# Even layer of a residual trunk: rounded products for the input projection, conditioning columns on TensorE's column groups, and a shared convolution

## The chip, the cores and the metric

The kernel runs on one core of a Trainium2 chip. The core has TensorE (matrix products into PSUM; PE in the profile, with its weight loads apart as PEld), VectorE (DVE), ScalarE (ACT), GpSimd (POOL) and SyncE (SP), whose queue issues the weight transfers. The metric is the device time of one execution in microseconds (us), the median of several runs; less is better.

## The reference

Two residual layers over 256 tokens of 2048 features, all in float32. Each layer is conditioned by a vector c:

```python
c_act = jax.nn.silu(c)
for l in range(2):
    mod = c_act @ ada_w[l] + ada_b[l]          # ada_w[l]: 2048 x 12288
    shift1, scale1, gate1, shift2, scale2, gate2 = jnp.split(mod, 6, axis=-1)
    h = rms(x, norm1_g[l]) * (1 + scale1) + shift1
    mix = even_mixer(h, ...) if l % 2 == 0 else mla_mixer(h, ...)
    x = x + gate1 * mix
    h = rms(x, norm2_g[l]) * (1 + scale2) + shift2
    x = x + gate2 * (square(relu(h @ mlp_w1[l])) @ mlp_w2[l])
```

The even mixer (layer 0) projects h by a matrix of 2048 x 4096 and splits the result into u, v, a, g of 1024 columns. Mixer A gates u by a 128 x 128 causal product over v. Mixer B takes a * sigmoid(g), a causal depthwise convolution of 31 taps over 1024 channels, a LayerNorm and a swish. Both results go through one output projection of 2048 x 2048. The odd mixer (layer 1) is attention with low-rank queries and keys. The change is in the even layer and the conditioning that it needs.

## The kernel before

The weights stream from memory as tiles of 1 MiB (128 partitions x 2048 floats) through four buffers named `raw`, in the order in which the program asks for them. For almost all products a tile is split: ScalarE casts it to a rounded value `wh` (line 94), VectorE forms the rest `wl` (line 95), and TensorE adds up three rounded products, high by high, low by high and high by low (lines 183 to 185, and 210 to 212 at the start of an MLP). The activations are kept as such pairs too.

The input projection of the even layer is the exception. `gemm32` (line 153) takes the raw tile and the activations `x` as whole float32, one product for each block of 128 features, 128 tokens and 512 columns. Its tiles go through the `wh` buffers, so that seven 1 MiB buffers are open to transfers there. The program first brings the columns of shift1 and scale1, four quarters of 512 features each; as soon as a quarter is known, `norm_quarter` normalizes and transposes 512 features of x, and three of the eight column chunks (`pa`, `pg`, `pa1`) take them. The other five chunks follow, four tiles each.

The conditioning is work "beside the weight tiles": each weight tile calls `side_work`, which pops steps of one 1 MiB piece of `ada_w` from a queue at a given rate, and taps of the convolution.

- shift1 and scale1, and later shift2 and scale2, are column sums on VectorE (`ada_quarters`, line 269: four multiply-adds of 512 for each piece, into `accq`), then four transposes and a reduction.
- gate1 is a row (`ada_row` with `side`): ScalarE multiplies (line 302), GpSimd adds (line 303). The first quarter of shift2 and scale2 goes the same way (lines 263 and 265). The rest of shift2 and scale2 reaches into the start of the MLP, which waits for it quarter by quarter.
- The convolution is 248 multiply-adds of 256 tokens on VectorE (lines 540 and 542), read from a copy in PSUM, ten to a weight tile.

The order of the instructions on each engine is set by a scheduler that takes the program's steps as they become ready; the queues `ada_queue` and `conv_queue` set where the steps stand in the program. PSUM has eight banks: four for products (`mm`), two for transposes (`tr`), two others (`ms`).

Of the kernel before, what the change touches and what calls it, by code (L numbers as in the profile page):

```python
# [36 lines left out]
R0, R1, R2, R4 = 1.2, 0.8, 0.75, 0.4  # L37
RA, NA = 2.5, 4
# [4 lines left out]
class Trunk:  # L43
    def __init__(self, ctx, tc, t):
# [12 lines left out]
        self.ms = pool("ms", 2, space=bass.MemoryType.PSUM)  # L57
# [4 lines left out]
        self.first = 0  # tiles still to be split by GpSimd  # L62
        self.conv_rate = 10
        self.conv_y = {}
        self.quarters = {}

# [1 line left out]
    def rsqrt(self, out, v):  # L68
        """out = v ** -0.5 for v > 0: a first guess from the bits, a third-order step, a Newton step."""
# [14 lines left out]
        # out <- 8/3 of its third-order step, then Newton with the 8/3 taken out again  # L84
# [7 lines left out]
    def split(self, src, hi, lo, engine=None):  # L92
        """src = hi + lo, both with the 12 significant bits that one pass of the array takes."""
        self.nc.scalar.copy(hi, src)  # L94
        (engine or self.nc.vector).tensor_tensor(lo, src, hi.bitcast(F32), op=ALU.subtract)  # L95
# [6 lines left out]
    def transpose4(self, srcs):  # L102
        """Up to four [128, n] blocks -> one PSUM bank, transposed side by side."""
# [20 lines left out]
    def wtile(self, w, k0, nk, n0, nw):  # L124
# [3 lines left out]
        # VectorE is busy with the norm when a phase's first tiles come: GpSimd splits those  # L128
# [6 lines left out]
    def side_work(self, size=1.0):  # L135
        """Work that is spread beside the weight tiles: conditioning and the convolution."""
# [7 lines left out]
        for _ in range(min(self.conv_rate, len(self.conv_queue))):  # L144
            self.conv_queue.pop(0)()

    def gemm32(self, ps, x, w, g, n0):
        """ps += x[:, 512 features of group g] @ w[those, n0:n0+512], whole float32 passes."""
        raw = self.wraw(w, 4 * g, 4, n0, 512, whole=True)
        self.side_work()  # L150
        for h in range(NH):
            for k in range(4):
                self.nc.tensor.matmul(  # L153
                    ps[h], x[:, 4 * g + k, h * P : (h + 1) * P], raw[:, k, :],
                    start=g + k == 0, stop=4 * g + k == KB - 1,
                )
# [68 lines left out]
    def ada_col(self, layer, j):  # L225
        """self.mod[layer, j] = [128, 16], feature-major."""
# [19 lines left out]
    def ada_quarters(self, layer, j0, side=None, aided=0):  # L246
        """Columns j0 and j0 + 1 side by side, complete for 512 features after every eight steps.
        The first aided quarters go by ScalarE and GpSimd, with room for products in side."""
# [3 lines left out]
        def step(q, g, i):  # L252
            if (q, g, i) == (0, 0, 0):
                box["acc"] = self.tmp.tile([P, 2, 2, 512], F32, tag="acc", name="accq", bufs=1)
                for j in (j0, j0 + 1):
                    self.mod[layer, j] = self.const.tile([P, KB], F32, tag=f"mod{layer}{j}", name=f"mod{layer}{j}")
            acc = box["acc"][:, q % 2, i, :]
            raw = self.wraw(self.t["ada_w"][layer], 4 * g, 4, (j0 + i) * D + q * 512, 512)
            for k in range(4):
                c = self.cT[:, 4 * g + k : 4 * g + k + 1]  # L260
                if q < aided:
                    prod = acc if g + k == 0 else side[:, D + k * 512 : D + (k + 1) * 512]
                    nc.scalar.activation(prod, raw[:, k, :], AF.Copy, scale=c)
                    if g + k:
                        nc.gpsimd.tensor_tensor(acc, acc, prod, op=ALU.add)
                elif g + k == 0:
                    nc.vector.tensor_scalar(acc, raw[:, k, :], c, None, op0=ALU.mult)
                else:
                    self.last = nc.vector.scalar_tensor_tensor(acc, raw[:, k, :], c, acc, op0=ALU.mult, op1=ALU.add).ins  # L269
            if g == 3:  # L270
                self.ada_finish_col(self.mod[layer, j0 + i], layer, j0 + i, q, acc)
                if i == 1:
                    self.quarters[layer, j0] = q + 1
# [4 lines left out]
    def ada_row(self, layer, j, side=None):  # L278
        """self.mod[layer, j] = [128, 2048], the same in every partition. With side = [128, 4096],
# [744 lines left out]
```

## Time and profile before

| what | us |
|---|---|
| median of 3 runs (2189.74 to 2189.92) | 2189.75 |
| span of the profiled execution, first to last instruction | 2185.9 |
| what lies around the span, against the median | 3.85 |
| conditioning and three chunks, up to the last quarter of features | 0 to 132.45 |
| the rest of the input projection | 132.45 to 297.80 |
| mixers and output projection | 297.80 to 411.20 |
| start of the MLP of layer 0, up to its second matrix | 411.20 to 523.70 |
| the rest: MLP of layer 0, layer 1 | 523.70 to 2185.9 |

The mean granted TensorE clock is 0.987 of full speed. In the profile's rows the first number is a start or a busy time, as the sentence ahead says; "x4" counts instructions; an arrow in brackets names what the engine waited for. A float32 product is shown as two records of TensorE and two of its weight load, a rounded product as one of each. Where a row says "idle before", an engine that doesn't set the end may idle at no cost.

### The profile page before, as it was taken

The numbers are of one execution on the slowest core, as the hardware profiler recorded it, in microseconds if no ns is written. First come the engines' busy times: TensorE is split into PE (matmuls) and PEld (weight loads), VectorE is DVE, ScalarE is ACT, GpSimd is POOL, SyncE is SP. The second block draws the span as 40 slices with busy tenths as digits, with TensorE's granted clock in tenths as the row PEclk, the third lists the DMA queues.
The fourth block names the chain that finished last, engine by engine and source line by source line (L and its number), as shares of the span: only waits on it lengthen the run. The fifth ranks groups of instructions, "written<-read, shape, count | busy, mean of one in ns | idle before, by whom it ended". The sixth has DMA issues, their size and how long they took to land.

```text
span 2185.9 us, 23655 instructions
## 1 busy us (share of the span) xinstructions
PE 2090.9 (96%) x9138; PEld 1635.7 (75%) x9138; DVE 1564.9 (72%) x1763; ACT 932.3 (43%) x1184; POOL 146.7 (7%) x95
## 2 busy tenths in 40 slices
PE   2889999899999999999998999989999999999999
PEld 1444458678888888888888787868888888888887
DVE  6849999888777878787767878766656545554555
ACT  2135435444444334333436776444434433433432
POOL 0038710000000000000001000010000000000000
PEclk9999999899999999999999999989999999999999
DMA  9999968899898899989755646647778556556653
GB/s 350 384 346 330 332 242 295 275 317 339 315 337 315 329 326 319 339 304 334 270 174 174 211 158 214 229 154 250 256 271 264 178 192 189 189 192 192 189 191 122
DMA packets 238620, 567.70 MB, mean 260 GB/s; under 512 B 9150, under 2 KB 17784, under 8 KB 221864
## 3 DMA queue, kind: packets, MB, share of 16 engines
q1 hardware_dynamic: 236288, 562.60, 74.3%
q10 hardware_dynamic: 1564, 2.28, 0.3%
q8 instruction: 72, 1.18, 0.2%
q0 software_dynamic: 656, 1.31, 0.2%
q14 instruction: 40, 0.33, 0.0%
HBM read 564.06 MB, written 2.10 MB: 259 GB/s over the span
## 4 chain that ended last, share of the span: by engine, by line
PE 85%; DVE 9%; DMA 5%; ACT 1%; issue 1%; SPq 0%; ACTq 0%; DVEq 0%
PE mm L183 23%; PE mm L184 23%; PE mm L185 23%; PE mm L153 4%; DMA raw<-in_ada_w 4%; PE trp L107 3%; DVE accq L269 2%; DVE cvsq L542 1%; DVE wl L95 1%; PE mm L210 1%; PE mm L211 1%; PE mm L212 1%; PE sc L797 1%; PE sc L796 1%; DMA raw<-in_mlp_w 1%
## 5 line engine op out<-in xcount | busy, mean ns | idle before, releaser
L95 DVE TENSOR_TENSOR wl<-raw,wh 128x2048 fp32r<-128x2048 f32 (+2 forms) x312 | 704.7, 2259 | 424.0 <-PE mm L184 317.9
L94 ACT CAST wh<-raw 128x2048 fp32r<-128x2048 f32 (+3 forms) x316 | 596.6, 1888 | 774.1 <-PE mm L185 515.2
L183 PE MATMUL mm<-wh,f_h 128*128 128x512 f32 x1024 | 399.6, 390 | 0.0
L185 PE MATMUL mm<-wh,f_l 128*128 128x512 f32 x1024 | 399.3, 390 | 0.0
L184 PE MATMUL mm<-wl,f_h 128*128 128x512 f32 x1024 | 398.7, 389 | 0.0
L185 PE MATMUL mm<-wh,h_l 128*128 128x512 f32 (+2 forms) x928 | 358.2, 386 | 0.0
L183 PE MATMUL mm<-wh,h_h 128*128 128x512 f32 (+2 forms) x928 | 358.2, 386 | 0.0
L184 PE MATMUL mm<-wl,h_h 128*128 128x512 f32 (+2 forms) x928 | 357.0, 385 | 0.6 <-DVE wl L95 0.6
L185 PEld LDWEIGHTS mm<-wh,f_l 128*128 128x128 f32 x1024 | 192.2, 188 | 39.8
L184 PEld LDWEIGHTS mm<-wl,f_h 128*128 128x128 f32 x1024 | 192.3, 188 | 39.6
L183 PEld LDWEIGHTS mm<-wh,f_h 128*128 128x128 f32 x1024 | 192.3, 188 | 39.2
L184 PEld LDWEIGHTS mm<-wl,h_h 128*128 128x128 f32 x928 | 175.0, 189 | 34.0 <-DVE wl L95 1.1
L185 PEld LDWEIGHTS mm<-wh,h_l 128*128 128x128 f32 x928 | 174.9, 188 | 33.4
L183 PEld LDWEIGHTS mm<-wh,h_h 128*128 128x128 f32 x928 | 175.0, 189 | 32.7
L153 PE MATMUL mm<-raw,x 128*128 128x512 f32 x448 | 195.7, 596 | 1.0 <-ACT x L500 0.6
L269 DVE SCALAR_TENSOR_TENSOR accq<-raw,cT,accq 128x512 f32<-128x512 f32 x210 | 153.7, 749 | 16.6 <-DMA raw<-in_ada_w 13.3
L153 PEld LDWEIGHTS mm<-raw,x 128*128 128x128 f32 x448 | 84.6, 191 | 104.6 <-issue 98.5
L237 DVE SCALAR_TENSOR_TENSOR acc<-raw,cT,acc 128x2048 f32<-128x2048 f32 x60 | 140.8, 2346 | 9.7 <-DMA raw<-in_ada_w 9.7
L297 DVE SCALAR_TENSOR_TENSOR acc<-raw,cT,acc 128x2048 f32<-128x2048 f32 x48 | 112.7, 2347 | 4.4 <-DMA raw<-in_ada_w 4.4
L542 DVE SCALAR_TENSOR_TENSOR cvsq<-yp,convw,cvsq 128x256 f32<-128x256 f32 x240 | 96.0, 476 | 0.0
L303 POOL TENSOR_TENSOR side<-side 128x1024 f32<-128x1024 f32 x32 | 74.8, 2361 | 19.3 <-ACT side L302 19.3
L452 ACT ACTIVATE relu<-mm 128x512 f32<-128x512 f32 x60 | 35.8, 599 | 87.7 <-PE mm L185 81.5
(270 smaller groups left out, 2246.9 us busy)
## 6 DMA issues: line engine op xcount, KB each, us to landing
raw<-in_mlp_w SPq DMA_DIRECT2D x256, 1024.0 KB, 5.6
raw<-in_ada_w SPq DMA_DIRECT2D x192, 1024.0 KB, 5.4
raw<-in_ab_w_in SPq DMA_DIRECT2D x32, 1024.0 KB, 9.7
raw<-in_ab_w_out SPq DMA_DIRECT2D x16, 1024.0 KB, 8.3
raw<-in_mla_w_out SPq DMA_DIRECT2D x16, 1024.0 KB, 4.9
raw<-in_mla_w_ukv SPq DMA_DIRECT2D x8, 1024.0 KB
raw<-in_mla_w_uq SPq DMA_DIRECT2D x8, 768.0 KB, 4.8
raw<-in_mla_w_in SPq DMA_DIRECT2D x4, 1024.0 KB, 7.2
```

What stands on the lines that cost most here:

```text
L94: self.nc.scalar.copy(hi, src)
L95: (engine or self.nc.vector).tensor_tensor(lo, src, hi.bitcast(F32), op=ALU.subtract)
L107: self.nc.tensor.transpose(ps[:w, i * P : i * P + s.shape[0]], s, self.ident[: s.shape[0], : s.shape[0]])
L153: self.nc.tensor.matmul(ps[h], x[:, 4 * g + k, h * P : (h + 1) * P], raw[:, k, :], start=g + k == 0, stop=4 * g + k == KB - 1,)
L183: nc.tensor.matmul(o, a, hi[:, i, :nw], start=first, stop=False)
L184: nc.tensor.matmul(o, a, lo[:, i, :nw], start=False, stop=False)
L185: nc.tensor.matmul(o, b, hi[:, i, :nw], start=False, stop=last)
L237: nc.vector.scalar_tensor_tensor(acc, raw, self.cT[:, kb : kb + 1], acc, op0=ALU.mult, op1=ALU.add)
L269: self.last = nc.vector.scalar_tensor_tensor(acc, raw[:, k, :], c, acc, op0=ALU.mult, op1=ALU.add).ins
L297: nc.vector.scalar_tensor_tensor(acc, raw, c, acc, op0=ALU.mult, op1=ALU.add)
L303: nc.gpsimd.tensor_tensor(acc[:, sl], acc[:, sl], prod, op=ALU.add)
L542: nc.vector.scalar_tensor_tensor(o, y, wk, o, op0=ALU.mult, op1=ALU.add)
```

## The change

- **Input projection.** `x` becomes a pair of rounded tensors, and all 32 tiles of the matrix are split and go through the three rounded products, as everywhere else. `gemm32` goes away. The tiles now pass through the four `raw` buffers.
- **scale1.** Of each quarter, the shift column stays on VectorE. The scale column is made on TensorE: a piece of `ada_w` is the moving operand of four float32 products, one for each block of 128 features, with the conditioning broadcast to 32 stationary columns, so that each product fills 32 partitions of one PSUM bank. ScalarE copies the bank, and small float32 products sum it up into columns and add the bias.
- **shift2 and scale2.** `ada_col_pe` does the same for whole columns, 16 pieces each, one after the other in bank `ms1`. The quarters and their waits at the start of the MLP go away. The steps stand at a rate of 1.5 to a weight tile: the 16 of shift2 between those of gate1, then the 16 of scale2.
- **Convolution.** Of the eight channel blocks, six stay on VectorE, with the sum in PSUM bank `ms0` and eight taps to a weight tile. The last two go to ScalarE (products) and GpSimd (sums of 512), two steps to a tile.
- The output projection starts two chunks instead of three with mixer A's rows, since the `ms` banks are in use; the LayerNorm is written ahead of them.

```diff
-        x = self.act.tile([P, KB, T], F32, tag="act", name="x0")
-        side = self.act.tile([P, 2 * D], F32, tag="act", name="side")
-        self.ada_more(8 / 3, self.ada_quarters(layer, 0))
+        x = self.act_pair(KB, "x0")
+        self.ada_more(RA, self.ada_quarters(layer, 0))
...
-            self.gemm32(pa, x, w, q, 2 * DA)
-            self.gemm32(pg, x, w, q, 3 * DA)
-            self.gemm32(pa1, x, w, q, 2 * DA + 512)
+            self.norm_quarter(quarter, q, x)
+            self.gemm_quarter([(pa, w, 2 * DA, 512), (pg, w, 3 * DA, 512), (pa1, w, 2 * DA + 512, 512)], x, q, 0)
...
+        g1 = self.ada_row(layer, 2, sq.rearrange("p a b -> p (a b)"))
+        s2 = self.ada_col_pe(layer, 3) + self.ada_col_pe(layer, 4)
+        mixed = [step for two in zip(g1[:16], s2) for step in two] + [g1[16]] + s2[16:]
+        self.ada_more(RB, mixed)
...
+    def ada_col_pe(self, layer, j):
...
+        def step(kb):
+            raw = self.wraw(self.t["ada_w"][layer], kb, 1, j * D, D)
+            if kb == 0:
+                box["acc"] = self.bank(1)
+            acc = box["acc"]
+            for s in range(4):
+                nc.tensor.matmul(
+                    acc[32 * s : 32 * s + 32], self.cT[:, kb : kb + 1].broadcast_to([P, 32]),
+                    raw[:, s * 512 : (s + 1) * 512], start=kb == 0, stop=kb == KB - 1,
+                )
...
+            def aided(b, k):
+                prod = cv[:, b : b + 2, :] if k == 0 else self.tmp.tile([P, 2, T], F32, tag="t512", name="cvp")
...
+                        nc.scalar.activation(prod[:, i], y, AF.Copy, scale=wk)
+                if k:
+                    nc.gpsimd.tensor_tensor(cv[:, b : b + 2, :], cv[:, b : b + 2, :], prod, op=ALU.add)
...
-            pv = self.psum2()
-            for g in range(4):
-                self.gemm32(pv, x, w, g, DA + j * 512)
+            pv = self.gemm(x, 0, w, 0, KB, DA + j * 512, 512)
...
-        self.ada_until(lambda: (layer, 2) in self.mod and self.quarters[layer, 3] >= 1)
...
-        pss = [self.psum2(), self.psum2(), [self.ms.tile([P, 512], F32, tag="ms", name=f"ms{h}") for h in range(NH)]]
+        pss = [self.psum2(), self.psum2()]
```

How the instructions move, at three places. First TensorE in the remaining chunks of the input projection, before; `raw` is the weight tile and `x` the activations, each row four float32 products:

```order
L153 MATMUL mm_864<-raw,x_117 128x512 x4
L153 MATMUL mm_865<-raw,x_117 128x512 x4
L153 MATMUL mm_995<-raw,x_117 128x512 x4
L153 MATMUL mm_996<-raw,x_117 128x512 x4
L153 MATMUL mm_995<-raw,x_117 128x512 x4
```

The same place in the change, with a step of shift2 (line 307; `cT` is the conditioning, `ms_1041` the bank that sums it up):

```order
L180 MATMUL mm_1238<-wh,x_h 128x512
L181 MATMUL mm_1238<-wl,x_h 128x512
L182 MATMUL mm_1238<-wh,x_l 128x512
L307 MATMUL ms_1041<-raw,cT 32x512 x4
L180 MATMUL mm_1237<-wh,x_h 128x512
L181 MATMUL mm_1237<-wl,x_h 128x512
L182 MATMUL mm_1237<-wh,x_l 128x512
```

Each float32 product has become three rounded ones, and the four products of a column step stand together between two blocks.

Second, TensorE where gate1 is finished (`gps`, the sum over partitions) ahead of mixer B's LayerNorm, in the change (before, lines 311 and 312 stand there with nothing between them):

```order
L357 MATMUL gps<-gh,onesr 128x512
L358 MATMUL gps<-gl,onesr 128x512
L307 MATMUL ms_2382<-raw,cT 32x512
L357 MATMUL gps<-gh,onesr 128x512
L358 MATMUL gps<-gl,onesr 128x512
L357 MATMUL gps<-gh,onesr 128x512
L358 MATMUL gps<-gl,onesr 128x512
L307 MATMUL ms_2382<-raw,cT 32x512 x3
```

Steps of scale2 now stand between these products.

Third, ScalarE in mixer A's v chunks, in the change. `wh` is the cast of a weight tile, `cvsq<-raw,cT` a product of gate1 that GpSimd adds up, `cvp` a product of the convolution, `vu` and `vq` belong to mixer A:

```order
L101 CAST wh<-raw 128x2048
L586 ACTIVATE cvp<-ypad,convw 128x256 x4
L348 ACTIVATE cvsq<-raw,cT 128x1024 x2
L101 CAST wh<-raw 128x2048 x2
L612 ACTIVATE vu<-mm_1466 128x512
L614 ACTIVATE vq<-vu 128x512
L348 ACTIVATE cvsq<-raw,cT 128x1024
L612 ACTIVATE vu<-mm_1467 128x512
L348 ACTIVATE cvsq<-raw,cT 128x1024
```

Before, this queue held no casts here: TensorE read the raw tiles. Now every weight tile passes through it, between products that go on to GpSimd.

More of the change, by code (lines that the diff above doesn't have):

```diff
@@ L143, in side_work @@
             self.ada_queue.pop(0)[1]()
[L144 to L156, printed above, removed]
+        for queue, rate in self.conv_queue:
+            for _ in range(min(rate, len(queue))):
+                queue.pop(0)()
     def psum2(self):
@@ L253, in step @@
             if (q, g, i) == (0, 0, 0):
-                box["acc"] = self.tmp.tile([P, 2, 2, 512], F32, tag="acc", name="accq", bufs=1)
+                box["acc"] = self.tmp.tile([P, 2, 512], F32, tag="acc", name="accq", bufs=1)
                 for j in (j0, j0 + 1):
                     self.mod[layer, j] = self.const.tile([P, KB], F32, tag=f"mod{layer}{j}", name=f"mod{layer}{j}")
-            acc = box["acc"][:, q % 2, i, :]
             raw = self.wraw(self.t["ada_w"][layer], 4 * g, 4, (j0 + i) * D + q * 512, 512)
-            for k in range(4):
[L260 to L269, printed above, removed]
+            if i == 0:
+                acc = box["acc"][:, q % 2, :]
+                for k in range(4):
+                    c = self.cT[:, 4 * g + k : 4 * g + k + 1]
+                    if g + k == 0:
+                        nc.vector.tensor_scalar(acc, raw[:, k, :], c, None, op0=ALU.mult)
+                    else:
+                        self.last = nc.vector.scalar_tensor_tensor(acc, raw[:, k, :], c, acc, op0=ALU.mult, op1=ALU.add).ins
+                if g == 3:
+                    self.columns(layer, j0, 4 * q, acc, self.ones[:, :1])
+                return
@@ L427, in mlp @@
         self.hold = self.hold and layer > 0
[L429 removed]
+        started = [self.psum2(), self.psum2(), [self.bank(h) for h in range(NH)]]
         for q in range(4 + AHEAD):
```

127 lines of the change are left out of this document (77 added, 50 removed).

## The prediction

> **What bounds the kernel now.** I read the page from the top: the busy shares, then the chain that ended last, then the stretches of the even layer one by one, because the change touches nothing after it.
>
> ```profile
> span 2185.9 us, 23655 instructions
> PE 2090.9 (96%) x9138; PEld 1635.7 (75%) x9138; DVE 1564.9 (72%) x1763; ACT 932.3 (43%) x1184; POOL 146.7 (7%) x95
> PE 85%; DVE 9%; DMA 5%; ACT 1%; issue 1%; SPq 0%; ACTq 0%; DVEq 0%
> ```
>
> TensorE is busy 96% of the span and carries 85% of the chain. The busy time by stretches shows the one place where this does not hold; the columns are PE, PEld, DVE, ACT, POOL, granted clock, DMA share and GB/s. The cuts are mine: 132.45 us is the first product of the last quarter of features, 297.80 the end of the input projection, 411.20 the end of the output projection, 523.70 the first product of the MLP's second matrix.
>
> ```profile
> 30.00:132.45 102.45, 79.14 (x208) 37.39 (x208) 88.55 (x158) 9.22 (x26) 4.96 (x9) 0.95 1.04 378
> 132.45:297.80 165.35, 163.78 (x407) 73.93 (x408) 129.57 (x301) 80.15 (x107) 115.53 (x65) 1.00 0.88 318
> 297.80:411.20 113.40, 108.20 (x486) 88.23 (x484) 107.18 (x143) 50.97 (x53) 0.00 (x0) 0.95 0.84 293
> 411.20:523.70 112.50, 99.75 (x452) 80.88 (x453) 99.11 (x115) 49.83 (x66) 1.81 (x1) 0.94 0.86 296
> 523.70:2185.90 1662.20, 1639.06 (x7585) 1354.61 (x7583) 1126.47 (x1026) 733.52 (x914) 21.00 (x11) 0.99 0.71 241
> ```
>
> Up to 132 us the transfers are the limit (share 1.04, 378 GB/s), and TensorE waits a quarter of the time. From 132 us on TensorE has 163.78 of 165.35 us, at full clock. So **an edit is worth what it takes from TensorE after 132.45 us**, and costs what it puts there. Work taken from VectorE is worth nothing there by itself.
>
> **The products of the input projection.** The same stretches, for line 153 alone (the full float32 products):
>
> ```profile
> 30.00:132.45 102.45, 67.99 (x144) 28.38 (x144) 0.95 1.04 378
> 132.45:297.80 165.35, 159.46 (x368) 69.29 (x368) 1.00 0.88 318
> ```
>
> There are 256 products in the program, and 144 + 368 = 512 records: each float32 product is two weight loads and two passes. 368 records take 159.46 us, 0.433 us a pass, 0.867 us a product, and 184 of the 256 lie where TensorE is the limit. A rounded product is one pass; the MLP and the attention output show its step:
>
> ```profile
> 1439.65 0.39 PE L184 MATMUL mm<-wl,o_h 128*128 128x512 f32 x1
> ...
> 1450.08 0.39 PE L185 MATMUL mm<-wh,o_l 128*128 128x512 f32 x1
> 1459.32 1.08 PE L107 MATMUL trp<-ident,xn 128*128 128x128 f32 x4 [8.85 <-DVE xn L354]
> ```
>
> From the first to the second row are 46 steps in 10.43 us, 0.2267 us each. Three of them are 0.680 us. So 184 products go from 159.5 to 184 x 0.680 = 125.1 us: **-34.3 us**. The other 72 lie under the transfers and are worth nothing.
>
> **The column steps on TensorE.** After 132 us the change issues 32 of them (16 for the second shift, 16 for the second scale), each one four float32 products whose results are 32 partitions by 512, on four column groups. Nothing like that is in the trace. Its bounds: four products side by side, with nothing else, cost one full product, 0.867 us; one after the other they cost four, 3.47 us. To either comes the change of shape. The nearest row for that is the 64-row product of the attention scores among 128-row ones:
>
> ```profile
> 1259.64 0.59 PE L796 MATMUL sc<-ring,qbuf 128*128 128x256 f32 x2
> 1260.16 0.70 PE L797 MATMUL sc<-krT,qbuf 64*128 64x256 f32 x2
> 1260.78 0.49 PE L796 MATMUL sc<-ring,qbuf 128*128 128x128 f32 x2
> 1261.20 0.48 PE L797 MATMUL sc<-krT,qbuf 64*128 64x128 f32 x2
> 1261.62 0.50 PE L183 MATMUL mm<-wh,cT 128*128 128x512 f32 x1
> ```
>
> By 0.433 us per pass of 512 columns, two passes of 256 should take 0.43 and two of 128 should take 0.22. From start to start the last three take 0.62, 0.42 and 0.42: each change of shape adds 0.20 us. A step has two, in and out, since the new order keeps its four products together nearly everywhere: 0.40 us.
>
> Between 0.867 and 3.47 I choose by how the two passes stand. The records show load, pass, load, pass for each product, and both passes of one product need the same columns. If TensorE starts its passes in order, the second pass of a product waits until the first has left its columns, and only then can the next product's first pass go beside it. Eight passes then take five slots: 5 x 0.433 = 2.17 us, with the changes of shape 2.57 us. 32 x 2.57 = **+82.2 us**. The ends are 32 x 0.867 = 27.7 and 32 x 3.87 = 123.8 us.
>
> The Trainium skill, "TensorE: Matmul & The Clock Gate", section "Part 3: Packing small matmuls — row/col tiling", says that products on different tiles of the array overlap almost wholly, a span of one product plus about 4 ns for each further tile, and gives 2.38x for three column groups. By that rule a step is one product long. The same section says that matmuls start and end strictly in program order, which is what the five slots need. No row here shows column groups; the first rule is the rival below.
>
> **Smaller terms.** These rows carry them:
>
> ```profile
> 302.61 0.79 PE L311 MATMUL gps<-gh,onesr 128*128 128x512 f32 x1 [4.42 <-ACT gate L313]
> 307.96 1.12 PE L107 MATMUL trp<-ident,vu 128*128 128x128 f32 x4 [0.68 <-ACT gate L313]
> 313.56 1.05 PE L593 MATMUL pm<-vu,wsT 128*128 128x128 f32 x8
> 338.13 0.60 PE L107 MATMUL trp<-ident,accq 128*128 128x128 f32 x4
> 410.79 0.39 PE L185 MATMUL mm<-wh,cat_l 128*128 128x512 f32 x1
> 523.71 0.48 PE L183 MATMUL mm<-wh,f_h 128*128 128x512 f32 x1
> 1557.73 0.48 PE L183 MATMUL mm<-wh,f_h 128*128 128x512 f32 x1
> ```
>
> Turning finished rows into columns: 16 tiny float32 products for the second shift and scale, two passes of about 0.13 us (1.05 us for 8) each, 4.2 us; away go 32 transposes, about 0.11 us each by their steps, 3.5 us: **+0.7 us**. The waits for the gate between 297 and 308 us (4.42 + 0.68) now have column steps standing in them: **-5 us**. The MLP's start no longer carries unfinished conditioning on VectorE: from the last output product to the first product of the second matrix layer 0 takes 523.71 - 410.79 = 112.9 us, and layer 1, without that conditioning, 1557.73 - 1450.08 = 107.7 us: **-5.3 us**.
>
> Before 132 us a quarter of features brings 11 pieces of 1 MiB, 30.5 us at 378 GB/s. TensorE needs in it 24 x 0.680 = 16.3, four column steps of 2.57 = 10.3, eight transposes 0.9 and 16 tiny products 4.2: 31.7 us. It just passes the transfers, 1.2 us in each of three quarters: **+3 us** (rounded down).
>
> **What lies beside.** Each weight tile is now cast and split before TensorE may read it, where before it read the raw tile:
>
> ```profile
> L95 DVE TENSOR_TENSOR wl<-raw,wh 128x2048 fp32r<-128x2048 f32 (+2 forms) x312 | 704.7, 2259 | 424.0 <-PE mm L184 317.9
> L94 ACT CAST wh<-raw 128x2048 fp32r<-128x2048 f32 (+3 forms) x316 | 596.6, 1888 | 774.1 <-PE mm L185 515.2
> L542 DVE SCALAR_TENSOR_TENSOR cvsq<-yp,convw,cvsq 128x256 f32<-128x256 f32 x240 | 96.0, 476 | 0.0
> L303 POOL TENSOR_TENSOR side<-side 128x1024 f32<-128x1024 f32 x32 | 74.8, 2361 | 19.3 <-ACT side L302 19.3
> L265 POOL TENSOR_TENSOR accq<-accq,side 128x512 f32<-128x512 f32 x30 | 39.0, 1301 | 6.8 <-ACT side L263 5.1
> ```
>
> 20 tiles of the remaining input projection add 20 x 2.26 = 45 us to VectorE and 20 x 1.89 = 38 us to ScalarE. VectorE loses 54 of its 240 taps (26 us) to the other two and some 26 taps to the time after the projection. Its 129.57 us there become about 137, under TensorE's 165. GpSimd has 32 x 2.36 + 30 x 1.30 = 115 us, as before. All of this I cost at nothing but for the waits in between: ScalarE's queue now holds the casts behind products that wait for GpSimd, and TensorE waits for the casts. Between 0 and the 12.75 us that TensorE idles in 411 to 524 us, where it already reads split tiles, I take **+5 us**; if VectorE's cover were gone, a tile would cost its whole excess, and this term its upper end.
>
> Sum: -34.3 + 82.2 + 0.7 - 5 - 5.3 + 3 + 5 = **+46.3 us** on the span of 2185.9. The median of the runs, 2189.75, lies 3.85 us above that span: 2236 us.
>
> **The rivals.**
> - *Four columns at the price of one.* If the passes of a step do run side by side, a step is 0.867 + 0.40 = 1.27 us and 32 are 40.6: -34.3 + 40.6 + 0.7 - 5 - 5.3 + 5 = +1.7 us, **2191 us**. For it: the groups share no columns. Against it: two passes per product on the same columns.
> - *Faster.* The same, and the change of shape costs nothing, since 64 rows are not 32 columns, and no tile is waited for: -34.3 + 27.7 + 0.7 - 5 - 5.3 = -16 us, **2173 us**. It decides as soon as a step is under 1.2 us and the split keeps up. Against it: the 0.20 us at every change of shape above.
> - *One after the other.* 3.87 us a step: 123.8 instead of 82.2, and a quarter of the prologue then takes 36.9 us for 30.5 of transfers, 19 us more in three: +104 us, **2294 us**. For it: no pass of this trace overlaps another.
> - *ScalarE and GpSimd as the bound.* Casts stuck behind gate products: 3 us a tile on 20 tiles, by GpSimd's 2.36 us, would be +60 on any of these. Against it: ScalarE and GpSimd have 80 and 116 of 165 us.
>
> **How the numbers follow.** Five slots: 0.45, around 2236, 2220 to 2250. Side by side: 0.27, 2180 to 2205. One after the other, or GpSimd on top: 0.16. Faster: 0.12. The range 2180 to 2288 holds the first two and the lower part of the third. About 0.2% (4.4 us) is what can be told from no change: the faster case with a quarter of the second gives 0.2 faster, half of the second 0.13 the same, the rest 0.67 slower. With both signs open, the likeliest case's own range is 2220 to 2250.
>
> **What would show it.** Three products a block at 0.227 us; the start-to-start time of a column step among ordinary products: 2.6, 1.3 or 3.9 us; the input projection still ending near 300 us and the output projection 40 us later than 411; the first product of the second matrix some 46 us later than 523.7, and the same distance from there to the end. It is wrong if a step is under 1.5 us, or if TensorE idles more than 15 us between 132 us and the MLP.

## The result, and the profile after

The changed kernel takes 2273.66 us (median of four runs, 2267.43 to 2277.40), the kernel before in the same comparison 2189.74 us: a ratio of 1.038, 95% interval 1.036 to 1.040. It is slower by 3.8%. The profiled execution of the changed kernel is the quickest of its four, 2267.43 us with a span of 2265.7 us; the sums below are made against spans, 2265.7 against 2185.9 us, **+79.8 us**.

The page of the changed kernel, its span, busy shares and the chain of waits:

```profile
span 2265.7 us, 25061 instructions
PE 2136.0 (94%) x9874; PEld 1706.3 (75%) x9874; DVE 1543.5 (68%) x1558; ACT 998.0 (44%) x1254; POOL 166.9 (7%) x95
PE 86%; DVE 7%; DMA 4%; ACT 2%; issue 1%; SPq 0%; DVEq 0%; ACTq 0%
```

TensorE has 45 us more work than before (2136.0 against 2090.9), but the span grew by 80. So nearly half of the loss isn't TensorE's work. The stretches show where it lies. The cuts are the same landmarks as in the prediction: first product of the last quarter of features, end of the input projection, end of the output projection, first product of the MLP's second matrix. The columns are again PE, PEld, DVE, ACT, POOL, granted clock, DMA share, GB/s.

```profile
30.00:166.54 136.54, 105.19 (x489) 68.54 (x481) 72.97 (x113) 33.77 (x55) 6.81 (x11) 0.91 0.83 298
166.54:367.81 201.27, 162.50 (x720) 114.62 (x720) 181.61 (x242) 115.54 (x142) 133.97 (x65) 0.92 0.77 278
367.81:497.50 129.69, 128.11 (x621) 89.19 (x620) 78.28 (x87) 56.97 (x62) 3.50 (x2) 0.99 0.82 298
497.50:603.16 105.66, 96.41 (x444) 79.28 (x445) 86.02 (x84) 50.10 (x64) 0.00 (x0) 0.95 0.81 280
603.16:2265.70 1662.54, 1638.59 (x7585) 1353.41 (x7583) 1115.45 (x1021) 733.07 (x913) 21.01 (x11) 0.99 0.69 237
```

| stage | before, us | after, us | difference |
|---|---|---|---|
| up to the last quarter of features (the prologue) | 132.45 | 166.54 | +34.1 |
| the rest of the input projection | 165.35 | 201.27 | +35.9 |
| mixers and output projection | 113.40 | 129.69 | +16.3 |
| start of the MLP | 112.50 | 105.66 | -6.8 |
| the rest | 1662.20 | 1662.54 | +0.3 |

In the prologue the transfers, which were the limit before at 378 GB/s, move only 298 GB/s. In the rest of the input projection TensorE, which worked 163.78 of 165.35 us before, works 162.50 of 201.27: the work is about the same, and 38.8 us are idle, 37.2 more than before. VectorE is now the busiest engine there, 181.61 us. Only the output projection is TensorE's own: 128.11 of 129.69 us.

**The column step is cheap.** The timeline of TensorE around one of the 32 steps, four products of two passes each:

```profile
202.57 0.39 PE L181 MATMUL mm<-wl,x_h 128*128 128x512 f32 x1
202.79 0.39 PE L182 MATMUL mm<-wh,x_l 128*128 128x512 f32 x1
203.11 1.06 PE L307 MATMUL ms<-raw,cT 128*32 128x512 f32 x8
204.11 0.50 PE L180 MATMUL mm<-wh,x_h 128*128 128x512 f32 x1
```

The product before the step would have made room after 0.227 us, at 203.02; the next one starts at 204.11. The step takes 1.09 us with both changes of shape, where the forecast had 2.57. Eight passes stand within 1.06 us, and by the 0.433 us of the prediction's float32 pass two of them alone are 0.867 us: the four products run side by side.

**What TensorE waits for** in the input projection after 166.54 us, its largest waits (PEld is its weight load), and with them ScalarE's for weight tiles (engine, line, what it waited for: us in total, times, longest):

```profile
PEld mm L181 <- DVE wl L102: 42.6, 13, 12.8
PE mm L181 <- DVE wl L102: 35.8, 8, 12.3
ACT wh L101 <- DMA raw<-in_ab_w_in: 35.3, 8, 14.7
```

TensorE waits for the second half of the split, on VectorE. The 12.3 us wait ends at 303.34. VectorE's own timeline before that, and GpSimd's beside it:

```profile
295.65 2.00 DVE L89 TENSOR_TENSOR nr<-nr 128x16 f32<-128x16 f32 x1
297.57 0.48 DVE L576 SCALAR_TENSOR_TENSOR ms<-ypad,convw,ms 128x256 f32<-128x256 f32 x1
297.96 1.99 DVE L97 SCALAR_TENSOR_TENSOR rv<-nr,rv 128x16 f32<-128x16 f32 x1
299.87 3.41 DVE L102 TENSOR_TENSOR wl<-raw,wh 128x2048 fp32r<-128x2048 f32 x1
303.20 17.07 DVE L621 SCALAR_TENSOR_TENSOR vu<-vu,rv,sgug 128x128 f32<-128x128 f32 x16
```

```profile
295.26 4.65 POOL L349 TENSOR_TENSOR acc<-acc,cvsq 128x1024 f32<-128x1024 f32 x2
299.87 11.36 POOL L588 TENSOR_TENSOR cvsq<-cvsq,cvp 128x512 f32<-128x512 f32 x7
311.18 4.77 POOL L349 TENSOR_TENSOR acc<-acc,cvsq 128x1024 f32<-128x1024 f32 x2
```

An instruction of 16 columns takes 2.0 us, four times as long as a tap of 256 columns, and ends about when an addition of GpSimd ends. 16 products of 128 columns take 1.07 us each. The taps, which have one operand in PSUM, keep their 0.48 us. Nearly all that is held up has both operands in SBUF, as the split has; of the instructions with one operand, two of 16 columns are slow too (line 617 with 1.48 us, line 79 with 0.94). The reading that GpSimd holds VectorE up was tested first.

### The profile page after: what moved, and what is told of

It is laid out like the page before. It is cut to its first block, busy times and chain, and to the rows that moved or that the text cites. A ratio compares the mean times of both kernels' runs of the same rounds, so it can differ in the third digit from the quotient of the medians.

```text
span 2265.7 us, 25061 instructions
## 1 busy us (share of the span) xinstructions
PE 2136.0 (94%) x9874; PEld 1706.3 (75%) x9874; DVE 1543.5 (68%) x1558; ACT 998.0 (44%) x1254; POOL 166.9 (7%) x95
## 4 chain that ended last, share of the span: by engine, by line
PE 86%; DVE 7%; DMA 4%; ACT 2%; issue 1%; SPq 0%; DVEq 0%; ACTq 0%
PE mm L180 24%; PE mm L181 23%; PE mm L182 23%; PE trp L114 3%; DVE wl L102 3%; DMA raw<-in_ada_w 2%; PE mm L207 2%; PE mm L208 1%; PE mm L209 1%; DMA raw<-in_ab_w_in 1%; DVE ms L576 1%; PE ms L307 1%; PE ms L208 1%; PE ms L209 1%; PE ms L207 1%; ACT wh L101 1%
## 5 line engine op out<-in xcount | busy, mean ns | idle before, releaser
L102 DVE TENSOR_TENSOR wl<-raw,wh 128x2048 fp32r<-128x2048 f32 (+1 forms) x344 | 789.4, 2296 | 485.3 <-PE mm L181 327.2
L101 ACT CAST wh<-raw 128x2048 fp32r<-128x2048 f32 (+1 forms) x348 | 657.3, 1890 | 833.4 <-PE mm L182 545.8
L181 PE MATMUL mm<-wl,x_h 128*128 128x512 f32 x160 | 66.1, 413 | 35.9 <-DVE wl L102 35.8
L349 POOL TENSOR_TENSOR acc<-acc,cvsq 128x1024 f32<-128x1024 f32 x32 | 86.0, 2705 | 59.8 <-ACT cvsq L348 56.2
L576 DVE SCALAR_TENSOR_TENSOR ms<-ypad,convw,ms 128x256 f32<-128x256 f32 x174 | 84.8, 488 | 4.7
L338 POOL MEMSET acc<- 128x2048 f32 x4 | 7.2, 1807 | 1028.7 <-DVE mod L218 609.9
L181 PEld LDWEIGHTS mm<-wl,x_h 128*128 128x128 f32 x160 | 31.3, 195 | 50.4 <-DVE wl L102 42.6
```

What stands on the lines that cost most here:

```text
L181: nc.tensor.matmul(o, a, lo[:, i, :nw], start=False, stop=False)
L349: nc.gpsimd.tensor_tensor(acc[:, sl], acc[:, sl], prod, op=ALU.add)
L576: nc.vector.scalar_tensor_tensor(o, y, wk, i, op0=ALU.mult, op1=ALU.add)
```

## The experiments

Times are medians of four runs; the ratios are to the kernel before, timed beside them, with their 95% intervals. In the diffs the changed kernel is the base unless another is named.

### GpSimd's additions left out

```diff
@@ ada_row, with side
-                    nc.gpsimd.tensor_tensor(acc[:, sl], acc[:, sl], prod, op=ALU.add)
@@ aided
-                if k:
-                    nc.gpsimd.tensor_tensor(cv[:, b : b + 2, :], cv[:, b : b + 2, :], prod, op=ALU.add)
```

> The changed kernel with GpSimd's 62 additions left out: the 32 sums of the first gate's rows and the 30 sums of the convolution's blocks 6 and 7 (so the gate and two blocks are wrong; everything else is computed as in the changed kernel, ScalarE's products included). Theory 'late splits': behind the 166.5 us mark TensorE has 162.5 us of work in 201.3 us and waits for VectorE's subtraction of the split, which takes 2.80 us a tile while GpSimd adds, against 2.26 us a tile elsewhere; without the additions a tile falls back to 2.1 to 2.3 us, the small VectorE instructions with it, and the stage of 201 us shrinks to 160 to 170: 2235 to 2245 us against 2273.7. Rival 'amount of work': VectorE simply has too much to do, and GpSimd does not slow it; a tile stays at 2.8 us and the time falls by less than 10 us. Rival 'TensorE's own work': column steps and products set the stage; less than 5 us.

Measured: 2236.84 us, 1.0232 (1.0206 to 1.0257), 37 us less, as 'late splits' had it. The projection stage of this run, whole and for the splits alone (VectorE's busy time and count), and the groups of VectorE up to 620 us (busy, mean ns):

```profile
177.26:345.50 168.24, 160.25 (x720) 113.33 (x720) 146.96 (x242) 115.30 (x142) 3.68 (x3) 0.96 0.91 333
177.26:345.50 168.24, 52.95 (x23) 0.00 (x0) 0.96 0.91 333
```

```profile
L102 DVE TENSOR_TENSOR wl<-raw,wh 128x2048 fp32r<-128x2048 f32 x72 | 165.1, 2295 | 74.1 <-ACT wh L101 38.4 <-issue 9.2 <-PE mm L181 9.1
L575 DVE SCALAR_TENSOR_TENSOR ms<-ypad,convw,ms 128x256 f32<-128x256 f32 x174 | 85.0, 488 | 4.7
L618 DVE SCALAR_TENSOR_TENSOR vu<-vu,rv,sgug 128x128 f32<-128x128 f32 x16 | 4.3, 348 | 0.0
```

The same groups of the changed kernel:

```profile
L102 DVE TENSOR_TENSOR wl<-raw,wh 128x2048 fp32r<-128x2048 f32 x68 | 167.3, 2462 | 69.4 <-ACT wh L101 45.0 <-issue 8.1 <-ACT cvsq L348 4.4
L576 DVE SCALAR_TENSOR_TENSOR ms<-ypad,convw,ms 128x256 f32<-128x256 f32 x174 | 84.8, 488 | 4.7
L621 DVE SCALAR_TENSOR_TENSOR vu<-vu,rv,sgug 128x128 f32<-128x128 f32 x16 | 17.1, 1139 | 0.0
```

The stage shrinks from 201.3 to 168.2 us, near what TensorE needs (160.25). VectorE loses 34.7 us of busy time without one instruction less: the 23 splits of the stage 11.4 (64.32 to 52.95), the 16 products 12.8; the rest is mostly the small instructions of the same normalisation. The taps stay at 488 ns. So VectorE was held up, and TensorE with it. The run leaves open how: by GpSimd's work in SBUF, or because ScalarE, which waits for GpSimd to free a product's room, casts the next tile late.

### The same additions on a fixed tile

```diff
-                    nc.gpsimd.tensor_tensor(acc[:, sl], acc[:, sl], prod, op=ALU.add)
+                    nc.gpsimd.tensor_tensor(acc[:, sl], acc[:, sl], self.sgug, op=ALU.add)
@@ aided: the same, with the first 512 columns of self.sgug in place of prod
```

> The changed kernel with GpSimd's 62 additions kept in number and size, but adding a tile that never changes in place of ScalarE's products (so the first gate and two blocks of the convolution are wrong). GpSimd no longer waits for ScalarE, and ScalarE no longer for GpSimd to free a product's room. Leaving the additions out gave 2236.8 us, a split of 2.30 us instead of 2.80, and 168.2 us instead of 201.3 for the rest of the input projection; this run tells which of two effects that was. Theory 'one waits for the other': while GpSimd reads SBUF, VectorE's instructions with two operands in SBUF stand still; the additions are still there, a split stays at 2.7 to 2.9 us, the 16 products of the second normalisation near 1.07 us each, and the time is 2255 to 2275 us. Rival 'casts behind ScalarE's waits': the loss came from casts queued behind products that wait for GpSimd; without that wait 2235 to 2248 us.

Measured: 2269.62 us, 1.0373 (1.0356 to 1.0390). The projection stage, whole and for the splits alone:

```profile
171.07:372.20 201.13, 165.98 (x719) 117.08 (x719) 184.03 (x242) 115.69 (x142) 151.19 (x65) 0.91 0.76 279
171.07:372.20 201.13, 65.19 (x23) 0.00 (x0) 0.91 0.76 279
```

GpSimd now hardly waits (2.3 us ahead of all 62 additions), and ScalarE doesn't wait for it, yet the stage is 201.1 us again, and a split 2.83 us. The rival falls: it is the additions themselves.

### GpSimd writes only

```diff
-                    nc.gpsimd.tensor_tensor(acc[:, sl], acc[:, sl], prod, op=ALU.add)
+                    for _ in range(3):
+                        nc.gpsimd.memset(acc[:, sl], 0.0)
@@ aided: three memsets of cv[:, b : b + 2, :] in the same way
```

> The changed kernel with each of GpSimd's 62 additions replaced by three fills of the same tile with zero, which write SBUF and read nothing (so the first gate and two blocks of the convolution are wrong). By the fill of 128x2048 in 1.81 us the three take about 2.7 us for each addition of 128x1024 and 1.4 us for each of 128x512, so that GpSimd is as busy as before. If VectorE is held up by GpSimd's reading alone, a split falls to 2.1 to 2.4 us and the time to 2235 to 2248 us, as without additions; if any work of GpSimd in SBUF holds it up, the split stays at 2.7 us or more and the time at 2260 to 2275 us.

Measured: 2239.72 us, 1.0231 (1.0213 to 1.0249). The stage, and the splits alone; then GpSimd's two groups of the whole program:

```profile
172.62:342.25 169.63, 158.81 (x719) 112.47 (x719) 148.03 (x242) 115.20 (x142) 134.69 (x189) 0.97 0.90 331
172.62:342.25 169.63, 53.32 (x23) 0.00 (x0) 0.97 0.90 331
```

```profile
L350 POOL MEMSET acc<- 128x1024 f32 x96 | 89.6, 962 | 0.0
L590 POOL MEMSET cvsq<- 128x512 f32 x90 | 48.3, 536 | 4.5 <-ACT cvsq L585 1.9
```

GpSimd is as busy as in the changed kernel (134.69 against 133.97 us in the stage), yet a split takes 2.32 us and the stage 169.6. So it is GpSimd's reading that holds the splits up. Fills are not quite without effect: the 16-column instruction with one operand that took 1.48 us beside additions takes 1.04 beside fills, and 0.17 with neither; the runs leave open why. The Trainium skill, "SBUF — State Buffer", section "Who interferes with whom", states this rule: a VectorE instruction with two inputs in SBUF and a GpSimd instruction that reads SBUF exclude one another for a whole instruction, and one that only writes does not. For the splits the trace agrees, with 2.83 us a split beside reading additions and 2.32 beside fills. The forecast had both engines' work in the stage and did not weigh this.

### Column steps left out

```diff
@@ ada_col_pe, step
-            for s in range(4):
+            for s in range(4 if kb in (0, KB - 1) else 0):
```

> The changed kernel with 28 of the 32 column steps behind the prologue left out: of each column only the first and the last step's products stay, all loads stay (so the second shift and scale are wrong). By the trace a step takes 1.09 us from product to product with its changes of shape, 28 of them 30.5 us. 'Late splits': the 13 or so that lie in the input projection are hidden behind VectorE and give 0 to 5 us, the 15 or so in the output projection, where TensorE has 128.1 of 129.7 us, give their 16 us: 2250 to 2258 us. 'TensorE's own work': all 28 count, 2243 us by the trace's price, 2202 us by the forecast's 2.57 us a step.

Measured: 2265.33 us, 1.0356 (1.0331 to 1.0380): 8 us less for 28 steps, outside both expectations, and with an interval that overlaps that of the changed kernel. The projection and the output stage:

```profile
166.79:374.00 207.21, 155.46 (x609) 119.67 (x610) 184.22 (x242) 115.51 (x142) 132.72 (x65) 0.84 0.73 271
374.00:490.00 116.00, 111.07 (x509) 86.06 (x506) 77.98 (x87) 56.44 (x62) 3.45 (x2) 1.00 0.89 329
```

The output projection gains 13.7 us, about what was expected of it. The input projection gains nothing (207.2 against 201.3 us): TensorE only waits longer for the same splits. There the column steps cost nothing, because VectorE sets the time.

### The input projection back in float32

```diff
-        x = self.act_pair(KB, "x0")
+        x = self.act.tile([P, KB, T], F32, tag="act", name="x0")
...
-        pg = self.gemm(x, 0, w, 0, KB, 3 * DA + 512, 512)
+        pg = self.chunk32(x, w, 3 * DA + 512)
@@ all eight chunks go through the gemm32 of before
```

> The changed kernel with the whole input projection back in float32 products on raw tiles; the column steps and the shared convolution stay; everything is still computed. 'Late splits' and 'held buffers': nothing waits for a split, so the last quarter starts at 132 to 140 us, the rest of the projection is TensorE's 163.8 us plus some 15 column steps of 1.09 us, 180 us, and the end of it lies near 315 instead of 368 us; with the output projection as in the changed kernel the time is 2215 to 2230 us, in spite of 34 us more of products. 'TensorE's own work': the products come back at 34 us, 2300 us or more. The rest over 2189.7 us is then what the column steps and the shared convolution cost by themselves.

Measured: 2228.55 us, 1.0188 (1.0171 to 1.0205), inside the bounds of the first theory: although its products cost TensorE some 27 us more in the stage (164.13 us against the 137.2 worked out in the next section), the kernel is 45 us quicker than the changed one. The stages themselves came later than expected: the last quarter starts at 144.90 us (132 to 140 expected), and the projection ends at 326.10 (315). The projection stage, whole and for the column steps alone (PE, PEld):

```profile
144.90:326.10 181.20, 180.95 (x518) 74.74 (x517) 131.11 (x227) 79.59 (x127) 115.42 (x66) 0.99 0.86 317
144.90:326.10 181.20, 15.97 (x120) 2.35 (x120) 0.99 0.86 317
```

This prices a step where TensorE does set the time: 15 steps of 1.065 us are 15.97 us, and the stage is 15.85 us longer than before the change. GpSimd adds here too (115.42 us), but nothing in the stage waits for a split. What remains over the kernel before, 37.7 us on the spans, is 15.9 here, 15.9 in the output stage (with 17 more column steps), a prologue that is 12.5 us longer, less 6.7 at the MLP's start.

### The prologue's products in float32, and then in the raw buffers

The first edit takes the products of the three early chunks back to float32, with the tiles in the `wh` buffers as before the change. The second differs from it by one word.

```diff
-            self.gemm_quarter([(pa, w, 2 * DA, 512), (pg, w, 3 * DA, 512), (pa1, w, 2 * DA + 512, 512)], x, q, 0)
+            for ps, n0 in ((pa, 2 * DA), (pg, 3 * DA), (pa1, 2 * DA + 512)):
+                self.gemm32(ps, full, w, q, n0)
@@ and, in the second run, inside gemm32
-        raw = self.wraw(w, 4 * g, 4, n0, 512, whole=True)
+        raw = self.wraw(w, 4 * g, 4, n0, 512)
```

> The changed kernel with the products of the first three chunks (the ones that run while the first conditioning is loaded) back in whole float32, read from raw tiles that lie in the buffers of the high halves, as before the change; everything is still computed. Theory 'held buffers': the prologue is 34 us longer because its 12 weight tiles are held in the four raw buffers until they are split, so that the loads behind them start late (298 GB/s against 378); with them out of the raw buffers the last quarter starts at 132 to 140 us instead of 166.5, and the time is 2240 to 2250 us. Rival 'crowded prologue': the column steps and the tiny products keep TensorE back there (105 us busy against 79), and the float32 products add some 20 us to that: the last quarter starts no earlier than 165 us, 2270 us or more.

> As the run with the prologue's products in float32 (2255.5 us, last quarter from 148 us), with one difference: the twelve weight tiles lie in the four buffers of the conditioning's pieces, as in the changed kernel, and not in those of the high halves; no split stands before these products. Everything is computed. Theory 'held buffers': a tile keeps its buffer until TensorE has used it, the loads behind it start late, and the last quarter starts at 160 to 170 us as in the changed kernel: 2266 to 2278 us. Rival 'the split itself': the cast and the subtraction ahead of every product made the prologue longer, and buffers play no part: 145 to 150 us, 2250 to 2260 us.

Measured: 2255.50 us, 1.0314 (1.0291 to 1.0336), with the last quarter from 149.98 us; and 2278.65 us, 1.0407 (1.0385 to 1.0428), with the last quarter from 164.25 us (inside the bounds of 'held buffers'; the time is 0.7 us over them). The stretch up to there, first of the one, then of the other:

```profile
30.00:149.98 119.98, 110.90 (x413) 54.06 (x405) 49.95 (x97) 13.19 (x38) 4.09 (x6) 0.94 0.92 336
```

```profile
30.00:164.25 134.25, 114.92 (x412) 55.44 (x405) 50.23 (x98) 13.19 (x38) 3.82 (x5) 0.91 0.83 295
```

One word costs 14.3 us in the prologue of these two profiles, and 23 us in all. The weight tiles then share the four `raw` buffers with the pieces instead of having three of their own, and the transfers move 295 GB/s instead of 336; the split by itself adds little (166.54 against 164.25). But with the buffers as before, the prologue is still 17.5 us longer than 132.45, and the first run missed both of its ranges (132 to 140 us for the last quarter, 2240 to 2250 for the time). TensorE's 110.90 of 119.98 us fit the rival's crowding, as a second cause. SyncE's waits in the run with all products in float32, where the prologue was 12.5 us longer, point to it:

```profile
SPq L125 <- PE adap L288: 47.6, 12, 7.9
SPq L125 <- DVE accq L279: 20.9, 6, 7.0
```

`adap` is the first scale's column step: its piece is given back only when TensorE, in its order, has come to it. The mixed version below makes this column on VectorE, as before the change, and its last quarter starts at 134.43 us, so that the column on TensorE costs the prologue some 15 us. Whether it does so by the late pieces or by the 30 us of work that it puts on TensorE there (110.90 against 80.67) was not separated. (The changed prologue itself varies: in seven profiled kernels in which it is unaltered the last quarter starts between 165.6 and 177.3 us. The parts named here are rough by as much.)

### The convolution not shared

```diff
@@ glu
-                    if b == 6:
+                    if b == 99:
```

> The changed kernel with the last two blocks of the convolution back on VectorE, like the other six; everything is computed. VectorE gains 62 taps of 0.49 us, 30 us, in a stage where it is busy 181.6 of 201.3 us; GpSimd loses its 30 additions, 46 of its 131 us, and with them about a third of the 33 us that all additions cost, 11 us. 'VectorE paces the projection': some 15 us slower, 2280 to 2295 us. Rival 'the additions cost more than the taps they save': 2250 to 2270 us, and the sharing would be a loss by itself.

Measured: 2272.99 us, 1.0388 (1.0372 to 1.0403), no difference from the changed kernel. The two stages:

```profile
165.59:346.80 181.21, 160.43 (x719) 114.99 (x720) 160.39 (x242) 91.02 (x80) 88.54 (x35) 0.93 0.86 309
346.80:501.30 154.50, 134.43 (x621) 92.31 (x619) 108.01 (x149) 57.07 (x62) 3.60 (x2) 0.91 0.71 250
```

The input projection is 20 us shorter and the output stage 25 us longer: VectorE has 149 instructions there instead of 87, since 62 taps that no longer fit beside the tiles stand ahead of the LayerNorm. TensorE's longest waits there are for pieces of `ada_w` (15.1 us in five); how the taps bring them about was not followed. The sharing moves the work and gains nothing; neither theory had this.

### The second normalisation's products spread

```diff
-                nc.vector.scalar_tensor_tensor(
+                self.conv_queue[2][0].append(lambda h=h, g=g: nc.vector.scalar_tensor_tensor(
...
-        self.conv_queue = [([], 8), ([], 2)]
+        self.conv_queue = [([], 8), ([], 2), ([], 3)]
```

> The changed kernel with the 16 products of the second normalisation, which stand in one piece of 17 us before the splits of two weight tiles on VectorE's queue, given out three to a weight tile over the next six tiles. Everything is computed. 'One waits for the other' and VectorE pacing the stage: TensorE's waits of 12.3 and 10.9 us go, but their work stays on a queue that is busy 181.6 of 201.3 us: 10 to 18 us faster, 2256 to 2264 us. Rival 'only the place of the wait': the same work delays other splits, 2268 to 2278 us.

Measured: 2267.59 us, 1.0361 (1.0342 to 1.0381), 0.4 us below the rival's bounds and outside the theory's, with an interval that overlaps that of the changed kernel. The stage stays at 201.7 us and TensorE's longest waits at 11.82 and 6.53 us. On this queue, busy 178.36 us of the stage, moving the work gained nothing that the runs can show.

### A version between the two

```diff
@@ from the version with the prologue's products in float32
-        self.ada_more(RA, self.ada_quarters(layer, 0))
+        self.ada_more(RA, self.ada_quarters32(layer, 0))
-        s2 = self.ada_col_pe(layer, 3) + self.ada_col_pe(layer, 4)
-        mixed = [step for two in zip(g1[:16], s2) for step in two] + [g1[16]] + s2[16:]
-        self.ada_more(RB, mixed)
+        s2 = self.ada_col_pe(layer, 3)
+        mixed = [step for two in zip(g1[:16], s2) for step in two] + [g1[16]] + self.ada_col(layer, 4)
+        self.ada_more(1.4, mixed)
@@ ada_quarters32 is ada_quarters of before; the products are spread as above
```

> A version between the two, computing everything: the prologue as before the change (first shift and scale on VectorE, first three chunks in float32 products, here of the tile from which the halves are split); the other chunks as three rounded products; the second shift by column steps on TensorE beside the input projection, the second scale on VectorE beside the output projection, where VectorE has 78 of 130 us; convolution shared as in the changed kernel; the 16 products of the second normalisation spread over the tiles that follow, three to a tile. By the theory the prologue ends near 133 us, the rest of the projection lies between the 168 us without GpSimd's additions and the 201 us with them, 185 us, the output projection loses its column steps and takes 113 us, the MLP's start 106 us, the rest 1662 us: 2199 us on the span, 2203 us, and 2186 us at best. If it is over 2230 us, the places named so far aren't where the time goes.

Measured: 2250.02 us, 1.0281 (1.0266 to 1.0296): quicker than the changed kernel, 47 us over its expectation and no match for the kernel before. It is over the 2230 us from which, as the expectation says, the places named so far don't account for the time. Its first three stretches:

```profile
30.00:134.43 104.43, 80.67 (x204) 37.41 (x205) 93.11 (x169) 9.53 (x26) 1.68 (x1) 0.93 1.01 369
134.43:338.10 203.67, 170.04 (x692) 114.94 (x692) 170.91 (x233) 112.52 (x145) 138.19 (x73) 0.90 0.76 274
338.10:475.30 137.20, 117.32 (x501) 91.09 (x500) 117.70 (x119) 57.48 (x60) 8.07 (x4) 0.90 0.81 288
```

The prologue is back. The gain is given back right behind it: GpSimd still adds for most of the 203.67 us, 20 splits take 59.20 us there (2.96 each), and the second scale on VectorE brings that engine to 117.70 us in the output stage, where TensorE waits again. Which part of these waits is which was not separated, and so what the change would cost without its known faults stays open. No version that was run beats the kernel before.

## Why the prediction was right or wrong

The sign was right and the reason was not. The forecast of 2236 us (range 2180 to 2288) took the column steps for the loss; they take 35 to 39 us of TensorE instead of 82, and two terms that it held small, the prologue (+34.1) and TensorE's idle time in the projection (+37.2), hold most of the 80 us. That 2273.66 us lies in the range is luck: the column steps were put 43 us too high and the products, the prologue and the idle time together 75 us too low. The case held likeliest had 2220 to 2250.

- **The column steps, +82.2.** This step failed: "five slots" supposes that a product's second pass bars the next product. A step took 1.09 us beside products and 1.065 where it could be priced, below every estimate but the lowest bound of 0.867, and under the 1.5 us below which the prediction calls itself wrong. TensorE spends 39.3 us on 32 of them. The rival *four columns at the price of one*, 1.27 us, was right on the mechanism, and its change of shape was still too dear: what lies over 0.867 is 0.2 us for both changes, not 0.40. The prediction had taken the price from the last three of its four score rows; the first, 0.52 us for two passes of 256 columns, gives 0.09 us for a change, close to the 0.1 us measured. By the Trainium skill, "TensorE: Matmul & The Clock Gate", section "Part 3: Packing small matmuls — row/col tiling", a step is one product long; the trace agrees to within 0.2 us, with 1.065 against 0.867 us. Leaving that rule's result at a chance of 0.27, against an order of passes that no row showed, was the mistake.
- **The rounded products, -34.3.** Their step is as forecast, 202.57 to 202.79. In the stage their sum is 162.50 less 18.04 of column steps, 4.84 of transposes and 2.42 of mixer A's, 137.2 us instead of 125.1: a gain of 22 us. Runs of products that are broken by waits start again at half pace (below), which is some 6 of the 12 us that are missing; the others were not traced. And the gain on TensorE is worth nothing where TensorE waits.
- **Casts and splits, +5.** The term that failed most. The range for it came from the idle time of the MLP's start, where GpSimd does next to nothing (1.81 us). In the projection stage TensorE's idle time went from 1.6 to 38.8 us. The prediction's sum of VectorE's work, 137 us, priced a split by a mean over the whole program, 2.26 us. VectorE had 181.61 us; without GpSimd's additions it has 146.96, so 35 us of standing still were missing and 10 us of other work. (Of the taps, the two blocks that move are 60 of the 240 and not 54, which changes the sum by 3 us.) The sentence "it is wrong if TensorE idles more than 15 us between 132 us and the MLP" applies. The trace of the kernel before already showed the effect, in VectorE's small instructions beside GpSimd's additions:

```profile
245.37 4.70 POOL L303 TENSOR_TENSOR side<-side 128x1024 f32<-128x1024 f32 x2 [0.33 <-ACT side L302]
248.10 2.00 DVE L81 TENSOR_TENSOR nr<-rv 128x16 f32<-128x16 f32 x1
251.84 0.16 DVE L81 TENSOR_TENSOR nr<-rv 128x16 f32<-128x16 f32 x1
```

  Line 81 takes 2.00 us while GpSimd adds, and 0.16 us at the same shape in the pause before the next addition at 251.96. The change put splits, which also have two operands in SBUF, beside such additions.
- **The rival of casts behind gate products** names the right engine, GpSimd. Its size is too large (3 us a tile, 60 us; without the additions the stage is 33 us shorter, 1.4 us for each of 23 tiles), and its path is wrong: not ScalarE's queue (the fixed operand changed nothing), but VectorE's instructions with two operands in SBUF. "ScalarE and GpSimd have 80 and 116 of 165 us" was no argument against it; it is in GpSimd's busy time that VectorE is held up.
- **The prologue, +3.** It measured +34.1. The term balanced TensorE's work against the transfers and did not ask which buffer each tile holds and until when. By single profiles, some 14 us are the weight tiles in the four `raw` buffers, 12 to 17 us the first scale's column on TensorE, and the rest, a few us, the split.
- **Output and MLP start.** The MLP's start gained 6.8 us where 5.3 were forecast: right. The output projection grew by 16.3 us, with 21.23 us of column steps on TensorE, which works 128.11 of 129.69 us: here alone the forecast's view, that TensorE's work is the time, held. Its idle time there fell from 5.20 to 1.58 us, of the 5 us forecast for the waits for the gate.

## What to carry to other kernels

Before work is put on an engine that looks free, ask what it shares: here a second engine's reading of SBUF made a split about a fifth longer (2.80 us against 2.30), which the busy share of neither engine gives away. A term costed at nothing because another engine has room is to be priced in the stage where it runs, beside what runs there, not by a mean over the program. And when a tile changes the buffers that it goes through, follow each buffer to its release: the release by an engine that works in order can become a wait of the transfer queue.

## What the runs showed of the hardware

- A float32 product on 32 columns shares its time with three others on the other column groups, its two passes included: 1.065 us for four products of 512 columns and both changes of shape, against 0.867 us for one full product.
- GpSimd's reads of SBUF hold up VectorE's instructions with two operands in SBUF. The shorter the instruction, the worse: 16 columns 1.0 to 2.0 us instead of 0.17, 128 columns 1.139 instead of 0.348, 2048 columns 2.80 instead of 2.30. Instructions with one operand in PSUM keep their time (488 ns in both). GpSimd's additions are longer too: the seven of 512 columns shown above take 1.62 us each, those of the kernel before 1.30 in the mean.
- After a wait TensorE's passes come at half pace for a while. The clock granted in 297.00 to 303.34 us, the wait of the changed kernel, is 0.50, and the passes behind it are 0.43 us apart until 306.06:

```profile
303.34 0.80 PE L181 MATMUL mm<-wl,x_h 128*128 128x512 f32 x1 [12.34 <-DVE wl L102]
303.93 0.63 PE L182 MATMUL mm<-wh,x_l 128*128 128x512 f32 x1
304.35 0.63 PE L180 MATMUL mm<-wh,x_h 128*128 128x512 f32 x1
...
306.06 0.45 PE L181 MATMUL mm<-wl,x_h 128*128 128x512 f32 x1
306.35 0.39 PE L182 MATMUL mm<-wh,x_l 128*128 128x512 f32 x1
306.57 0.39 PE L180 MATMUL mm<-wh,x_h 128*128 128x512 f32 x1
```

A wait thus costs more than its length. Some 29 passes of the stage were that far apart, against 0.227 us at full pace, about 6 us in all.
